# A hybrid decoder step on one core: low-part products over all 128 partitions

## The chip, the core and the metric

The kernel runs on one core of one Trainium2 chip. TensorE (PE) multiplies, VectorE (DVE), ScalarE (ACT) and GpSimd (POOL) work on elements, and SyncE (SP) issues most transfers between DRAM and on-chip memory (SBUF). Each engine takes its instructions in a fixed order and waits on semaphores for the others. The metric is the device time of one execution in microseconds (us).

## The reference

One layer of a decoder with two parallel branches, for a prompt of 1024 tokens and 8 x 8 sample tokens that share the weights, all in float32, width 1024:

```
h = rmsnorm(x); p = h @ w_in
q, k, v, ga, ps, gb, ma, mb = split(p)
# branch A: attention, 16 heads of 64 in 4 key groups, window 128, bias by distance, one sink per head
s = q k^T * 64**-0.5 + bias (masked);  o = softmax with sink (s) v
ya = (o * silu(ga)) @ w_out_a
# branch B: RWKV-7, 16 heads of 64
z = ps + (prev - ps) * mu;  r, k, v, wl, al = split(z)
w_raw = -softplus(-(w0 + tanh(wl) @ w2)) - 0.5        # rank 64
a     = sigmoid(a0 + al @ a2)                          # rank 64
per token:  S = S * decay + (S at) bt + v k;  y = S r
yb = (groupnorm(y) + bonus) * silu(gb) @ w_out_b
out = rmsnorm(x + (sigmoid(ma) * ya + sigmoid(mb) * yb) @ w_o)
```

Key and value windows, the RWKV states and the last shifted rows are returned too.

## The kernel before

Channels lie on the 128 partitions and tokens along the free axis, in chunks of 364, 364 and 360 columns. A float32 operand is split into a high part that the fast matmul format (fp32r) holds exactly and a low part, the rest. A dense product takes three passes into one PSUM region: high by high, high by low, low by high (`mm3`, shown as `d` in the profile: `whi`, `wlo` are the weights' parts, `hhi`, `hlo` those of h, `yhi`, `ylo` those of the RWKV output, `oh`, `ol` those of the attention output).

The program has these stages. `start` norms the input, with constants loaded through POOL's queue: `con` (identity, epsilons, masks, scan pattern, all in one tile of 728 columns), `prm` and others. `rwkv` runs about 16 units of 256 tokens by two groups of heads: `quarter` does the element work of a group (`lo`, `kn`, `bo`, `A`, `t` products), `invert` a triangular inversion on DVE (`TM`, `TR`, `Tt`), `chain` the recurrence (`c`, `y`, `q` products), `samples` the sample tokens (`ss`; `ve` is a masked copy for the state update, made with the scan constants of `con`), `posts` the group norm (`gc` with the centring matrix `cen`, `gv` with the block sums `bone`). Dense projections fill PE between them. `attention` follows, and `final` does the output projections (`wo`).

The order on PE is written by a planner (`drive`): each stream is a generator that stops before products that must wait; the planner keeps an estimated clock, advanced in `mm` by columns alone, and goes on with the first stream whose operands should be there. Dense products are the last stream and fill the rest. Within the RWKV stage and within attention this order is kept on PE; the other engines' orders, and how the end of one stage mixes with the start of the next, come from the framework's scheduler. Buffers are tiles of pools laid out in SBUF end to end in the order in which the pools open: constants, weights, then RWKV elements, chain and post; the attention pools open where the RWKV pools stood. A tile that takes the place of others waits for their last use.

*Attention.* For a pair of heads (e = 0, 1, one on each half of the partitions) `att_keys` loads the keys `kT` and writes for each head a tile `ks` with the high part of its keys on both halves (ACT, L1027 and L1028), and one tile `klo` with the low parts, each head's in place on its own half (DVE, L1029). `q_split` makes for each head a tile `qs` with the query's high part on the head's half and its low part on the other. Thus one product over 128 rows gives (q high + q low) times k high, and a second over the 64 rows of the head's half adds q high times k low. `att_half` runs 2 blocks of 128 queries at a time: eight score products (`s`), softmax on DVE and ACT (`sc`, with the eviction from PSUM at L1126, the exponential at L1052, the scaling at L1056), transposes (`pt`), products with values (`o`, values by token in `vtok`, made by the transposes `vt` of `vT`), and the gate. Two halves of the blocks run as separate streams, for eight pairs of heads.

*Low-rank projections.* The tiles `zs` hold for each token the rank-64 vector's high part on one half of the partitions and its low part on the other; the weights `w2` stand twice, on both halves, and are split into `w2h` and `w2l`. One product over 128 rows takes w2h with both parts, a second over the 64 rows of the high part adds w2l with it.

Of the kernel before, what the change touches and what calls it, by code (L numbers as in the profile page):

```python
# [42 lines left out]
# tile numbers in the stacked weight array  # L43
# [11 lines left out]
# columns of the shape constants  # L55
C_ID = 0
C_MI = 128
C_MS = 192
C_SI = 256
C_SS = 320  # L60
C_SEQ = 384
C_SCAN = 392
C_EPS = 724
NCONST = 728

# columns of the per-channel parameters
# [15 lines left out]
class Prog:  # L82
# [6 lines left out]
    # ---------------------------------------------------------------- helpers  # L89
# [6 lines left out]
    def cst(self, col, n, lo=0, hi=P):  # L96
        return self.con[lo:hi, col:col + n]

    # ---------------------------------------------------------------- PE order
    def mm(self, out, lhsT, rhs, transpose=False, **kw):  # L100
        """a product, and its estimated time"""
        n = 1
        for d in rhs.shape[1:]:
            n *= d
        if transpose:
            self.nc.tensor.transpose(out, lhsT, rhs)  # L106
        else:
            self.nc.tensor.matmul(out, lhsT=lhsT, rhs=rhs, **kw)  # L108
        self.clk += n / 2400 if rhs.dtype == F32R else n / 1200 if lhsT.shape[-1] > 64 else n / 1700
# [22 lines left out]
    def ready(self, st):  # L132
        """estimated time at which a stream's next products have their operands"""
        if st[2] is not None:
            if st[2] not in self.marks:
                return None
            st[2], st[3] = None, self.marks[st[2]] + st[3]
        return max(st[3], self.free.get(st[4], 0.0))

    def drive(self, streams):  # L140
        """products are issued in the order of emission: of the streams (generators that stop ahead of products
        that have to wait for other engines) the first one whose operands should be there goes on"""
        live = [[gen, off, None, 0.0, None] for gen, off in streams]
        while live:
            best = None
            for st in live:
                t = self.ready(st)
                if t is not None and (best is None or t < best[0] - 1e-9) and not (best and best[0] <= self.clk):
                    best = (t, st)
            assert best, ("no stream can go on", [(st[0].__name__, st[2]) for st in live], self.marks.keys())  # L150
            t, st = best
            self.clk = max(self.clk, t)
            if not self.step(st):
                live.remove(st)
# [17 lines left out]
    def chunk_tiles(self, stack, nm):  # L172
        """hi and lo parts of a [P, KT, NT] operand, a pool for each chunk"""
        hi, lo = [], []
        for c0, c1 in CHUNKS:
            pool = stack.enter_context(self.pool(f"{nm}{c0}", side="right"))
            hi.append(pool.tile([P, KT, c1 - c0], F32R, name=f"{nm}hi{c0}"))
            lo.append(pool.tile([P, KT, c1 - c0], F32R, name=f"{nm}lo{c0}"))
        return hi, lo
# [20 lines left out]
    def dense2(self, ia, ib, rhi, rlo, ea, eb):  # L200
        """two tiles, chunk by chunk"""
        wa = self.pre.pop(ia)
        self.seq.remove(ia)
        self.seq.remove(ib)
        wb = self.load_w(ib)
        for ci, (c0, c1) in enumerate(CHUNKS):
            for j, (i, w, evac) in enumerate(((ia, wa, ea), (ib, wb, eb))):
                ps = self.ps(self.d3, f"d{i}_{ci}") if (2 * ci + j) % 3 == 2 else self.ps("d", f"d{i}_{ci}", 2)
                yield from self.mm3(ps[:, :c1 - c0], *w, rhi[ci], rlo[ci])
                evac(c0, c1, ps[:, :c1 - c0])  # L210
                if ci == 2 and j == 0:
                    self.pre[self.seq[0]] = self.load_w(self.seq[0])
                yield

    def sig_neg(self, out, tmp, src, scale, bias):
        """out = sigmoid(-(scale*src + bias)), by exp and ln of one table set"""
        nc = self.nc
        nc.scalar.activation(tmp, src, AF.Exp, scale=scale, bias=bias)
        nc.scalar.activation(tmp, tmp, AF.Ln, bias=1.0)
        nc.scalar.activation(out, tmp, AF.Exp, scale=-1.0)  # L220

    def load_split(self, pool, src, hi, lo, nm, bufs):
        """exact hi/lo parts of a float32 row of tiles in DRAM"""
        nc = self.nc
        t = pool.tile([P, NT], F32, tag="stage", name=f"stage{nm}", bufs=bufs)
        nc.sync.dma_start(t, src)
        nc.scalar.activation(hi, t, AF.Copy)  # L227
        nc.vector.tensor_tensor(lo, t, hi.bitcast(F32), ALU.subtract)  # L228
# [8 lines left out]
    def sum2(self, ps, w, parts):  # L237
        """ps = w^T (hi + lo) with w exact in fp32r: one pass for each part"""
# [3 lines left out]
    # ---------------------------------------------------------------- program  # L242
    def run(self):
        tc, nc = self.tc, self.nc
        nc.scalar.preload_act_table_set("natural_log_exp_and_others")
        with ExitStack() as top:
# [16 lines left out]
            self.con = cp.tile([P, NCONST], F32, name="con")  # L263
            self.prm = cp.tile([P, NPAR], F32, name="prm")
            self.prd = cp.tile([P, 52], F32, name="prd")
            self.bone = cp.tile([P, P], F32R, name="bone")
            self.cen = cp.tile([P, P], F32R, name="cen")
# [12 lines left out]
    def start(self, xp, w0):  # L280
        """the norm, chunk by chunk, with the first two projections"""
# [5 lines left out]
        self.zs = [ep.tile([P, NT], F32R, name=f"zs{j}") for j in range(2)]  # L287
        bc = xp.tile([P, 2, P], F32, name="bc")
        for t, i in ((self.con[:, C_MI:], self.I["con"][:, C_MI:]), (prm, self.I["par"]), (self.con[:, :C_MI], self.I["con"][:, :C_MI]),
# [95 lines left out]
    # ------------------------------------------------------------------ RWKV  # L385
    def shift_tile(self, idx, ti, out):
        """project one token-shifted tile; out(ci, c0, c1, z) takes z = ps + (prev - ps) * mu by chunks"""
# [49 lines left out]
    def spill(self, idx, dst, kind="copy", scale=1.0):  # L437
        """a projected tile, or its sigmoid or silu, sent to DRAM"""
# [105 lines left out]
    def front(self, s):  # L544
        """unit s: 256 tokens (and, with the last of them, the sample tokens) of two groups of two heads"""
# [31 lines left out]
    def quarter(self, g, q, gi, f):  # L577
# [10 lines left out]
        def v64(t):  # prompt chunks  # L588
            return t[:, :256].rearrange("p (c s) -> p c s", c=4)

        def s64(t):  # sample tokens by sequence
            return t[:, 256:320].rearrange("p (b s) -> p b s", b=NB)

        def d64(t, off, w=64):  # decay layout, prompt; off 1 = inclusive, 0 = exclusive
# [13 lines left out]
        # decay and in-context rate  # L608
        res = []
        pl = [self.ps("m", f"lo{nm}0"), self.ps("a", f"lo{nm}1", 2)]  # L610
        for j, r0 in enumerate((0, 64)):
# [3 lines left out]
            self.mm(ps[:, :n], lhsT=w2[1][r0:r0 + 64, j, :], rhs=self.zs[j][r0:r0 + 64, a0:a0 + n], start=False, stop=True)  # L615
# [18 lines left out]
        # normalised key  # L634
# [4 lines left out]
        # k' = k * (1 + (a - 1) * k_a)  # L639
# [18 lines left out]
        # bonus: v * sum(r * k' * r_k)  # L658
# [10 lines left out]
        # chunk arrays  # L669
# [67 lines left out]
    def invert(self, nm, n2, f):  # L737
        """tr[0:64] = ((I - A_ab)^-1)^T: 32 x 32 diagonal blocks by forward substitution, then merged.
        A block's columns lie on three partitions (columns 3c', 3c'+1, 3c'+2)."""
# [188 lines left out]
    # ------------------------------------------------------------- attention  # L928
# [46 lines left out]
    def att_load(self):  # L975
        """values by token, keys, and queries that were projected before"""
# [41 lines left out]
    def att_keys(self, m):  # L1018
        """keys of a pair of heads: hi parts on both halves of the partitions, lo parts in place"""
# [4 lines left out]
        self.klo = self.a0.tile([P, SEQ], F32R, tag="klo", name=f"klo{m}", bufs=1)  # L1024
        for e in range(2):
# [3 lines left out]
            nc.vector.tensor_tensor(self.klo[er], t[er, :SEQ], self.ks[e][er].bitcast(F32), ALU.subtract)  # L1029
# [5 lines left out]
    def q_split(self, qs, src, c0, c1, scale):  # L1035
        """queries: a head's hi parts on its half of the partitions, its lo parts on the other half"""
# [6 lines left out]
    def softmax4(self, sc, mx, sinkv, nu, nm, x):  # L1043
        """sc: [P, nu, w] scores with bias, mx: [P, nu] row maxima (sink included); normalised in place"""
# [44 lines left out]
    def att_half(self, x):  # L1089
        """half of the blocks of each pair of heads"""  # L1090
# [5 lines left out]
        for i in QORD:  # L1096
# [7 lines left out]
            for b0 in range(bq, bq + 4, 2):  # L1104
# [7 lines left out]
                for e in range(2):  # L1112
                    er = slice(e * 64, e * 64 + 64)
                    for bb in range(2):
# [6 lines left out]
                        self.mm(po, lhsT=qs[e][er, b * P:(b + 1) * P], rhs=self.klo[er, k0:k0 + w], start=False, stop=True)  # L1121
# [105 lines left out]
    # ---------------------------------------------------------------- output  # L1227
# [92 lines left out]
# ------------------------------------------------------------- host layouts  # L1320
def _chan(v, n):
    """[n*128] per-channel vector -> [128, n]"""
# [9 lines left out]
def _consts():  # L1332
# [22 lines left out]
    # block ones; block centering  # L1355
# [4 lines left out]
def prep(inp):  # L1360
# [45 lines left out]
    # [(twice, rank), g, decay | rate, channel]  # L1406
# [3 lines left out]
    # [b, h, v, k] -> [g, (h2, k), b, v]  # L1410
# [7 lines left out]
    # sample: rows (b4, g, i); columns 128 cached + 64 new (b, i)  # L1418
# [28 lines left out]
def finish(r):  # L1447
# [4 lines left out]
    def win(a):   # [m, (e, d), t] -> [t, kv, d]  # L1452
# [5 lines left out]
    # [g, k, (h2, v)] -> [h, v, k]  # L1458
    pw = np.ascontiguousarray(r["pwkv"].reshape(8, 64, 2, 64).transpose(0, 2, 3, 1)).reshape(1, 1, 16, 64, 64)
    # [g, (h2, k), b, v] -> [b, h, v, k]  # L1460
# [19 lines left out]
```

## Time and profile before

| | |
|---|---|
| time, median of 3 runs | 1918.33 us (1914.55 to 1920.26) |
| profiled execution, first to last instruction | 1909.7 us |
| PE busy | 1837.7 us (96%) |
| PE weight loads busy | 1617.2 us (85%) |
| DVE busy | 1117.7 us (59%) |
| ACT busy | 968.6 us (51%) |
| POOL busy | 359.6 us (19%) |
| mean granted PE clock | 0.991 |

The page of the profile has the span of the profiled execution, not a device time of its own; the runs lie 4.9 to 10.6 us above the span. A row of a group reads: line, engine, operation, out<-in, shapes, count, then total busy us, mean ns of one, and idle time of the engine before them. A row of the timeline reads: start, length, engine, line, operation, tiles, shapes, count. In shapes such as `64*128` the first number is the rows of the array that a product contracts over, the second its output rows. `PEld` rows are weight loads, which can run under products. Records of products overlap, so their starts tell the pace.

### The profile page before, as it was taken

Reading aid. Unit: us, or ns where it says so; the run is one execution under the profiler, and the core shown is the slowest. Engines: PE = TensorE matmul, PEld = TensorE weight load, DVE = VectorE, ACT = ScalarE, POOL = GpSimd, SP = SyncE. Lnnn points to the kernel's source line nnn. Section 1 sums busy time; section 2 is a strip of 40 time slices with the busy share of each in tenths; the row PEclk is TensorE's granted clock in tenths of the full one; section 3 lists DMA queues with packets and bytes.
Section 4 is the critical chain, followed back from the end, with each engine's and each line's share of the span. In section 5 each row is a group of like instructions: output and inputs, shape, how many; then the busy total and the mean of one; then the engine's idle time right before and its main releaser. Section 6 shows DMA issues by size and latency. Waiting matters only on the chain.

```text
span 1909.7 us, 35535 instructions
## 1 busy us (share of the span) xinstructions
PE 1837.7 (96%) x13056; PEld 1617.2 (85%) x13056; DVE 1117.7 (59%) x3243; ACT 968.6 (51%) x2442; POOL 359.6 (19%) x356
## 2 busy tenths in 40 slices
PE   6999999999999999999999999999999999999998
PEld 4998888888787888887888888897888888799997
DVE  6325757576567466577576567544555666544543
ACT  5456556464455563565564555434555754432232
POOL 4443222132133212123211021211100000000000
PEclk9999999999999999999999999999999999999999
DMA  4333332332333333242332332332411524274521
GB/s 157 110 115 118 101 80 87 104 103 85 92 98 91 96 84 92 74 123 81 102 100 80 94 116 77 103 93 90 152 51 50 171 92 123 78 234 138 180 104 59
DMA packets 180994, 199.42 MB, mean 104 GB/s; under 512 B 72052, under 2 KB 156388, under 8 KB 180788
## 3 DMA queue, kind: packets, MB, share of 16 engines
q1 hardware_dynamic: 180244, 194.19, 33.7%
q0 software_dynamic: 576, 2.96, 0.5%
q8 instruction: 103, 1.69, 0.4%
q14 instruction: 71, 0.58, 0.1%
HBM read 135.09 MB, written 63.95 MB: 104 GB/s over the span
## 4 chain that ended last, share of the span: by engine, by line
PE 46%; DVE 3%; ACT 1%; DMA 1%; issue 1%; POOL 0%; DVEq 0%; SPq 0%; POOLq 0%; ACTq 0%
PE d L108 24%; PE wo L108 5%; PE s L108 4%; PE y L108 2%; PE c L108 2%; PE o L108 2%; PE pt L106 1%; DMA stageo<-d_o 1%; DVE Tt L757 1%; PE A L108 1%; DVE TR L759 1%; PE t L106 0%; PE lo L108 0%; PE os L108 0%; PE ss_d L108 0%
## 5 line engine op out<-in xcount | busy, mean ns | idle before, releaser
L108 PE MATMUL d<-hhi,whi 128*128 128x364 f32 (+1 forms) x1656 | 571.3, 345 | 9.4 <-DVE gz L432 5.4
L108 PE MATMUL d<-hlo,whi 128*128 128x364 f32 (+1 forms) x1656 | 549.3, 332 | 7.9 <-DVE hlo L347 7.0
L108 PEld LDWEIGHTS d<-hhi,whi 128*128 128x128 f32 x1656 | 315.3, 190 | 31.9 <-issue 9.2
L108 PE MATMUL d<-hhi,wlo 128*128 128x364 f32 (+1 forms) x1656 | 333.4, 337 | 0.0
L108 PEld LDWEIGHTS d<-hlo,whi 128*128 128x128 f32 x1656 | 315.8, 191 | 11.3 <-DVE hlo L347 9.6
L108 PEld LDWEIGHTS d<-hhi,wlo 128*128 128x128 f32 x1656 | 276.8, 190 | 9.6 <-issue 4.5
L169 POOL TENSOR_TENSOR wlo<-wraw,whi 128x1024 fp32r<-128x1024 f32 x56 | 136.0, 2429 | 360.9 <-PE d L108 136.5
L757 DVE TENSOR_TENSOR Tt<-TM,TR 96x90 f32<-96x90 f32 (+26 forms) x496 | 150.2, 303 | 11.0
L759 DVE TENSOR_TENSOR TR<-TR,Tt 96x90 f32<-96x90 f32 (+26 forms) x496 | 133.7, 270 | 13.7 <-issue 1.2
L168 ACT ACTIVATE whi<-wraw 128x1024 fp32r<-128x1024 f32 x90 | 95.0, 1056 | 79.0 <-PE d L108 70.5
L402 POOL TENSOR_TENSOR zz<-zz,pad 128x364 f32<-128x364 f32 (+1 forms) x75 | 76.1, 1016 | 204.9 <-ACT zz L401 139.7
L1052 ACT ACTIVATE sc<-sc,st 128x256 f32<-128x256 f32 (+1 forms) x128 | 61.9, 486 | 50.0 <-DVE st L1048 50.0
L830 DVE COPY vsu<-c 64x256 f32<-64x256 f32 x64 | 27.4, 428 | 98.1 <-PE c L108 87.6
L108 PE MATMUL y<-am,vsu 128*64 128x64 f32 x512 | 81.4, 245 | 0.0
L108 PE MATMUL y<-tr,xs 64*64 64x64 f32 x480 | 77.9, 242 | 0.0
L1126 DVE CUSTOM_DVE_ANT_0 sc<-s,bias,prm 128x256 f32<-128x256 f32 (+1 forms) x128 | 55.7, 463 | 32.8 <-PE s L108 32.7
L400 ACT ACTIVATE pad<-d,prm 128x364 f32<-128x364 f32 (+1 forms) x75 | 40.8, 544 | 60.3 <-PE d L108 50.8
L1314 POOL TENSOR_TENSOR xr<-xr,frs 128x256 f32<-128x256 f32 x2 | 1.8, 932 | 368.0 <-ACT frs L1311 368.0
L108 PE MATMUL d<-yhi,whi 128*128 128x364 f32 (+1 forms) x192 | 65.0, 339 | 0.0
L108 PE MATMUL d<-oh,whi 128*128 128x364 f32 (+1 forms) x192 | 63.4, 330 | 0.7 <-ACT oh L227 0.5
L108 PE MATMUL d<-ol,whi 128*128 128x364 f32 (+1 forms) x192 | 63.2, 329 | 0.4 <-DVE ol L228 0.4
L108 PE MATMUL A<-RA,KB 64*128 64x128 f32 x544 | 63.5, 291 | 0.0
(308 smaller groups left out, 3626.6 us busy)
## 6 DMA issues: line engine op xcount, KB each, us to landing
wraw<-in_w SPq DMA_DIRECT2D x93, 512.0 KB
d_z<-zz SPq DMA_DIRECT2D x48, 182.0 KB
d_m<-sp SPq DMA_DIRECT2D x32, 182.0 KB
TM<-s SPq DMA_DIRECT2D x72, 64.0 KB
stageo<-d_o SPq DMA_DIRECT2D x8, 544.0 KB
d_z<-zz SPq DMA_DIRECT2D x24, 180.0 KB
w<-in_lora SPq DMA_DIRECT2D x32, 128.0 KB
bias<-in_biasp SPq DMA_DIRECT2D x16, 256.0 KB
```

Source lines behind the costliest of these rows:

```text
L106: self.nc.tensor.transpose(out, lhsT, rhs)
L108: self.nc.tensor.matmul(out, lhsT=lhsT, rhs=rhs, **kw)
L168: nc.scalar.activation(hi, raw, AF.Copy)
L169: (nc.vector if self.dve_lo else nc.gpsimd).tensor_tensor(lo, raw, hi.bitcast(F32), ALU.subtract)
L400: nc.scalar.activation(pad[:, 1:1 + m], ps[:, :m], AF.Copy, scale=mu)
L402: nc.gpsimd.tensor_tensor(z[:, :m], z[:, :m], pad[:, 0:m], ALU.add)
L757: nc.vector.tensor_tensor(tv, M[s // 16][:np_, s % 16:s % 16 + 1, s + 1:32].to_broadcast([np_, cc, w]), R[:np_, 0:cc, s:s + 1].to_broadcas ...
L759: nc.vector.tensor_tensor(R[:np_, 0:cc, s + 1:32], R[:np_, 0:cc, s + 1:32], tv, ALU.add)
L830: nc.vector.tensor_copy(vsu[up, c], pu)
L1052: nc.scalar.activation(sc[k], sc[k], AF.Exp, bias=st[:, 0, k:k + 1], accum_out=st[:, 1, k:k + 1])
L1126: nc.vector.tensor_tensor_reduce(sc[:, k, off:], ps[e][:, bb * 256 + off:bb * 256 + 256], bias[:, e, off:], 1.0, self.par(Q_SK + 4 * i + k ...
L1314: en.tensor_tensor(xt[:, dt, :n], xt[:, dt, :n], rst[:, :n], ALU.mult)
```

## The change

- The low keys get a tile for each head, `klo[e]`, with the low part on both halves of the partitions, and the second score product contracts over all 128 partitions of `qs[e]` and `klo[e]`.
- The second low-rank product contracts over all 128 partitions of `w2l` and `zs`.
- `con` keeps only the identity and the epsilons. Masks and scan constants move to a tile `rco`, and `rco`, `bone` and `cen` are now in the pool of RWKV elements, which ends with the RWKV stage. The order of the constant loads is `con`, `prm`, `rco`.

Comments and docstrings are dropped too. The core of the diff:

```diff
 C_ID = 0
-C_MI = 128
...
-C_SCAN = 392
-C_EPS = 724
+C_EPS = 128
+C_MI = 132
...
+C_SCAN = 396
 NCONST = 728
...
     def cst(self, col, n, lo=0, hi=P):
-        return self.con[lo:hi, col:col + n]
+        if col < C_MI:
+            return self.con[lo:hi, col:col + n]
+        return self.rco[lo:hi, col - C_MI:col - C_MI + n]
...
-            self.con = cp.tile([P, NCONST], F32, name="con")
+            self.con = cp.tile([P, C_MI], F32, name="con")
...
-            self.bone = cp.tile([P, P], F32R, name="bone")
-            self.cen = cp.tile([P, P], F32R, name="cen")
...
+        self.rco = ep.tile([P, NCONST - C_MI], F32, name="rco")
+        self.bone = ep.tile([P, P], F32R, name="bone")
+        self.cen = ep.tile([P, P], F32R, name="cen")
...
-        for t, i in ((self.con[:, C_MI:], self.I["con"][:, C_MI:]), (prm, self.I["par"]), (self.con[:, :C_MI], self.I["con"][:, :C_MI]),
+        for t, i in ((self.con, self.I["con"][:, :C_MI]), (prm, self.I["par"]), (self.rco, self.I["con"][:, C_MI:]),
                      (bc, self.I["bc"]), (self.shp, self.I["shift"])):
...
-        for j, r0 in enumerate((0, 64)):
+        for j in range(2):
...
-            self.mm(ps[:, :n], lhsT=w2[1][r0:r0 + 64, j, :], rhs=self.zs[j][r0:r0 + 64, a0:a0 + n], start=False, stop=True)
+            self.mm(ps[:, :n], lhsT=w2[1][:, j, :], rhs=self.zs[j][:, a0:a0 + n], start=False, stop=True)
...
-        self.klo = self.a0.tile([P, SEQ], F32R, tag="klo", name=f"klo{m}", bufs=1)
+        self.klo = [self.a0.tile([P, SEQ], F32R, tag=f"klo{e}", name=f"klo{m}{e}", bufs=1) for e in range(2)]
         for e in range(2):
...
-            nc.vector.tensor_tensor(self.klo[er], t[er, :SEQ], self.ks[e][er].bitcast(F32), ALU.subtract)
+            for r in (er, xr):
+                nc.vector.tensor_tensor(self.klo[e][r], t[er, :SEQ], self.ks[e][er].bitcast(F32), ALU.subtract)
...
-                        self.mm(po, lhsT=qs[e][er, b * P:(b + 1) * P], rhs=self.klo[er, k0:k0 + w], start=False, stop=True)
+                        self.mm(po, lhsT=qs[e][:, b * P:(b + 1) * P], rhs=self.klo[e][:, k0:k0 + w], start=False, stop=True)
```

More of the change, by code (lines that the diff above doesn't have):

```diff
@@ L56 @@
 C_ID = 0
-C_MI = 128
[L58 to L61, printed above, removed]
-C_SCAN = 392
-C_EPS = 724
+C_EPS = 128
+C_MI = 132
+C_MS = 196
+C_SI = 260
+C_SS = 324
+C_SEQ = 388
+C_SCAN = 396
 NCONST = 728
@@ L1112, in att_half @@
                 for e in range(2):
-                    er = slice(e * 64, e * 64 + 64)
                     for bb in range(2):
```

## The prediction

> **What bounds the kernel now.** I read the totals first, then the busy time by stage, then the groups by shape, and last the instructions in order of time.
>
> ```profile
> span 1909.7 us, 35535 instructions
> ...
> PE 1837.7 (96%) x13056; PEld 1617.2 (85%) x13056; DVE 1117.7 (59%) x3243; ACT 968.6 (51%) x2442; POOL 359.6 (19%) x356
> ```
>
> TensorE (PE) is occupied almost throughout and nothing else passes 60%. The stages say the same (columns: window, length, busy of PE, weight load, DVE, ACT, POOL, granted clock, DMA share, GB/s):
>
> ```profile
> 1000.00:1270.00 270.00, 265.11 (x2078) 229.73 (x2078) 165.03 (x499) 143.93 (x360) 51.83 (x47) 0.99 0.32 92
> ...
> 1340.00:1500.00 160.00, 158.98 (x1026) 135.75 (x1025) 89.41 (x328) 88.26 (x250) 3.54 (x5) 1.00 0.26 83
> ...
> 1670.00:1800.00 130.00, 128.86 (x778) 126.96 (x777) 63.57 (x98) 33.05 (x44) 0.00 (x0) 1.00 0.58 175
> ```
>
> So PE sets the time in the RWKV stage (to about 1340 us), in attention (1340 to 1672) and behind it, and a microsecond taken off PE's own sequence is a microsecond of the span unless another engine is late. What matters is therefore the distance between starts on PE, not the length of a record, since records overlap. Three groups by shape, then the attention scores of one step in order of time:
>
> ```profile
> L108 PE MATMUL s<-ks,qs 128*128 128x256 f32 x112 | 42.8, 382 | 0.0
> L108 PE MATMUL s<-klo,qs 64*128 64x256 f32 x112 | 42.6, 381 | 0.0
> ...
> L108 PE MATMUL gc<-shic,cen 128*128 128x256 f32 x24 | 6.8, 284 | 0.0
> ```
>
> ```profile
> 1407.33 0.39 PE L108 MATMUL o<-pt,vtok 128*64 128x128 f32 x4
> 1407.64 0.38 PE L108 MATMUL s<-ks,qs 128*128 128x256 f32 x1
> 1407.96 0.38 PE L108 MATMUL s<-klo,qs 64*128 64x256 f32 x1
> 1408.27 0.39 PE L108 MATMUL s<-ks,qs 128*128 128x256 f32 x1
> ...
> 1409.83 0.38 PE L108 MATMUL s<-klo,qs 64*128 64x256 f32 x1
> 1410.14 1.09 PE L106 MATMUL pt<-con,sc 128*128 128x128 f32 x8
> ```
>
> Eight score products take 2.50 us, 0.31 each. A product of the same 256 columns, also in two passes into one PSUM region, but with 128 rows in both passes, starts the next one after 0.12:
>
> ```profile
> 1257.34 0.28 PE L108 MATMUL gc<-shic,cen 128*128 128x256 f32 x1
> 1257.46 0.28 PE L108 MATMUL gc<-sloc,cen 128*128 128x256 f32 x1
> 1257.57 0.33 PE L108 MATMUL d<-hhi,whi 128*128 128x364 f32 x1
> ```
>
> The weight loads show why. The first two rows are loads of the scores, the others of that pair:
>
> ```profile
> 1407.95 0.18 PEld L108 LDWEIGHTS s<-klo,qs 64*128 64x128 f32 x1
> 1408.27 0.19 PEld L108 LDWEIGHTS s<-ks,qs 128*128 128x128 f32 x1
> ```
>
> ```profile
> 1257.34 0.19 PEld L108 LDWEIGHTS gc<-sloc,cen 128*128 128x128 f32 x1
> 1257.46 0.19 PEld L108 LDWEIGHTS d<-hhi,whi 128*128 128x128 f32 x1
> ```
>
> The load of gc's second pass begins at 1257.34, as the first pass starts: it is hidden. The load of a score's 64-row pass begins at 1407.95, 0.31 behind the start of the product before it: nothing overlaps. This happens at each change between 128 and 64 rows, in both directions.
>
> **The change part by part.** *Scores.* The low pass takes 128 rows instead of 64, so the alternation ends. The columns streamed stay 256 (the added rows add the product of the two low parts), and I take 0.12 for a step. The first step after the o products (64 columns wide, still another shape) keeps an exposed load. That price is seen here, where kn follows a 64-row product:
>
> ```profile
> 110.16 0.28 PE L108 MATMUL lo<-zs,w2h 128*128 128x256 f32 x1
> 110.37 0.38 PE L108 MATMUL lo<-zs,w2l 64*128 64x256 f32 x1
> 110.68 0.38 PE L108 MATMUL lo<-zs,w2h 128*128 128x256 f32 x1
> 110.99 0.38 PE L108 MATMUL lo<-zs,w2l 64*128 64x256 f32 x1
> 111.30 0.39 PE L108 MATMUL kn<-shik,bone 128*128 128x256 f32 x1
> 111.53 0.28 PE L108 MATMUL kn<-slok,bone 128*128 128x256 f32 x1
> ```
>
> kn's first pass takes 0.23 to the next start. A group of eight then takes 0.23 + 7 x 0.12 = 1.07 instead of 2.50; the full-row product behind it loses its own exposed load, 0.23 - 0.12, so 1.5 us per group. There are 32 groups (8 head pairs x 2 halves x 2). In 8 of them four of the eight products have 128 columns, for the first block of tokens:
>
> ```profile
> 1637.75 0.33 PE L108 MATMUL s<-ks,qs 128*128 128x128 f32 x1
> 1638.00 0.32 PE L108 MATMUL s<-klo,qs 64*128 64x128 f32 x1
> ```
>
> These step by 0.25 now, and I take 0.11 after (the pt row above: 8 transposes of 128 columns, 1.09 with the last one's 0.27 in it), which leaves 1.3. Sum: 24 x 1.5 + 8 x 1.3 = 46.4 us. Bounds: 0 if the load stays exposed, 32 x 1.6 = 51 if the first step came down too.
>
> *Low-rank projections.* From the first lo to kn's second pass are 1.37 us; five steps at 0.12 make 0.60. That is 0.77 for each of 32 quarters (8 groups x 4; a quarter of them has 320 columns, for which I take the same), 24.6 us. Bounds 0 and 26.
>
> *How much arrives at the end.* In attention, softmax has to lie between scores and transposes, and a shorter PE sequence eats its slack. Normalising one step's scores (DVE) ends here, against its transposes on PE, once early and once late in attention:
>
> ```profile
> 1401.54 1.14 DVE L1056 TENSOR_SCALAR sc<-sc,st 128x256 f32<-128x256 f32 x4
> ```
>
> ```profile
> 1648.62 0.55 DVE L1056 TENSOR_SCALAR sc<-sc,st 128x128 f32<-128x128 f32 x2
> ```
>
> ```profile
> 1649.81 0.38 PE L106 MATMUL pt<-con,sc 128*128 128x128 f32 x2
> ```
>
> Early, the result is there at 1402.68 and used at 1410.14, over 7 us later; the 1.4 us of one group between them is covered. Over the last two heads (from about 1628, six groups) the last result is made at 1649.17 and used at 1649.81: 0.6 of cover. There the step loses up to 1.4, but DVE also starts its evictions earlier, since both PSUM banks are full after 1.07 rather than 2.5 while four evictions of 0.48 follow; I charge half, 6 x 0.7 = 4 us (0 to 9). What is late next there is the DVE eviction with ACT's exponentials. In the RWKV stage PE does wait, some 35 us in pieces, the largest in total being (in total, times, longest)
>
> ```profile
> PE t L106 <- ACT vsu L734: 10.9, 4, 3.8
> ```
>
> These are local hand-overs that move along with PE; the chain from lo through ACT also begins 0.6 us earlier. I keep 9 tenths, 22 us (15 to 25).
>
> *Second low key tile.* Four more DVE subtractions:
>
> ```profile
> L1029 DVE TENSOR_TENSOR klo<-kT,ks 64x1024 fp32r<-64x1024 f32 x4 | 4.8, 1209 | 0.6 <-ACT ks L1027 0.5
> ```
>
> 4 x 1.21 = 4.8 us on DVE, two at about 1330 and two at about 1497. DVE is 56% busy in that stretch. At 1330 the last RWKV post-processing stands behind them on DVE, and PE's gv waits for it, so up to 2.4 us may show; without that neighbour nothing would.
>
> *Memory.* The constants' pool shrinks by 2384 + 1024 bytes a partition (RWKV columns of con, bone, cen) and the pool of RWKV elements grows by as much, so its other tiles stay where they were. Attention's first pool begins where the elements began, 3.4 KB lower, and its tiles now lie over other RWKV tiles. By the order of allocation, the first value stage (bytes 8448 to 12800) comes to lie on the RWKV masks and scan constants, which the last sample step (ve) still reads, and ks of head 0 (12800 to 16896) on bone and cen, which the last gv reads:
>
> ```profile
> 1312.89 0.52 SPq L983 DMA_DIRECT2D vT<-d_v  x1
> ```
>
> ```profile
> 1331.88 0.67 DVE L893 TENSOR_TENSOR ve<-vss,con 128x512 f32<-128x512 f32 x1
> ```
>
> ```profile
> 1338.07 0.60 PE L106 MATMUL vt<-con,vT 128*128 128x128 f32 x4
> ...
> 1341.62 0.41 PE L108 MATMUL gv<-slov,bone 128*128 128x320 f32 x1
> ```
>
> The load can go at 1332.6 instead of 1312.9, and the transposes want it at 1338.07: 5.5 us for issue and 544 KB, which may just do. Behind it on the SyncE queue stand weight loads and the biases. ks of head 0 would be written from 1342 on, four operations of 1.1 to 1.2 us before its scores at 1353: covered. I charge 2 us for this and the DVE work together (a gain of 1 to a loss of 8).
>
> *Start.* The first constants' load falls from 300 to 66 KB, the third grows to 298 KB; the same bytes move.
>
> ```profile
> 14.64 0.56 ACT L330 ACTIVATE rst<-ss,con 128x364 f32<-128x364 f32 x1 [1.04 <-PE ss L108]
> ```
>
> prm may come a little earlier, but the first user that PE sees is rst, which waits for PE and not for constants: nothing (0.5 either way). The masks are first used after 100 us.
>
> Sum: 46.4 - 4 + 22 - 2 = 62 us. The profiled span would be 1909.7 - 62 = 1848. The runs' median, 1918.33, is 8.6 over that span, launch and spread together, which I leave as it is: 1918 - 62 = 1856.
>
> **The rivals.** *A: softmax takes over.* PE's share of attention falls by 46 of 332 us, and DVE with ACT become the limit in more than the last two heads. For it: the late rows above. Against: 7 us of cover earlier, and DVE and ACT at 55 to 56%; the same work in 138 instead of 160 us is 65%. If half of the attention gain goes, and RWKV keeps 15: 1918 - 23 - 15 = 1880, between 1876 and 1900.
>
> [...]
>
> *C: slower, by the clock.* The score and low-rank stretches draw full-array work at more than twice the rate. The granted clock is 0.99 to 1.00 in the windows above; if the denser stream brought it below about 0.96, PE's 1700 us of full-rate work would lose the 62 us again, and at 0.94 the kernel would take 1918 - 62 + 0.06 x 1700 = 1958. Against: from 1670 to 1800 PE does nothing but 128-row products, weight loads busy 98%, at 1.00.
>
> **How the numbers follow.** Forecast as summed, gains of 42 to 78 us, 0.82; A 0.12; B 0.03; C 0.03. The upper gain, 78, is all of the two terms with their upper bounds; the lower end takes the unfavourable end of each charge (46 - 9 + 15 - 8 = 44). The range 1840 to 1876 holds the forecast's case. A difference under 0.3% (6 us) cannot be told from none here, as the three runs spread by 5.7. Faster: forecast and A, 0.94; same: B, 0.03; slower: C, 0.03.
>
> **What would show it.** Right: s and lo products all 128 rows with mean records near 0.28 us, starts 0.12 apart, PE busy near 1775, DVE up by 5, klo eight times. Attention shorter by 40 or more between its first score and its last o, RWKV by about 20. [...] Wrong it would be through a long PE wait between 1310 and 1355 of the old time (value stage, ks, or a weight load stuck behind them), or steps between 0.12 and 0.31.

## The result, and the profile after

The changed kernel takes 1870.51 us (median of four runs, 1865.87 to 1874.02) against 1918.40 for the kernel before; the ratio is 0.9745, with an interval of 0.9717 to 0.9772. That is 48 us less where 62 were forecast, and the time lies within the predicted range, 14 us above the forecast of 1856. Some 12 us are lost at one place, the hand-over from RWKV to attention (experiment 3 measures it).

The totals of the profiled execution, which took 1874.02 us:

```profile
span 1872.2 us, 35547 instructions
...
PE 1783.7 (95%) x13056; PEld 1610.3 (86%) x13056; DVE 1123.9 (60%) x3247; ACT 963.8 (51%) x2442; POOL 359.2 (19%) x356
```

The changed products as groups by shape:

```profile
L110 PE MATMUL s<-ks,qs 128*128 128x256 f32 x112 | 31.4, 309 | 0.0
L110 PE MATMUL s<-klo,qs 128*128 128x256 f32 x112 | 28.3, 281 | 0.0
...
L110 PE MATMUL lo<-zs,w2l 128*128 128x256 f32 x48 | 12.6, 285 | 0.0
...
L1033 DVE TENSOR_TENSOR klo<-kT,ks 64x1024 fp32r<-64x1024 f32 x8 | 10.3, 1288 | 1.7 <-ACT ks L1030 1.5
```

Eight scores in order of time, with the dense product behind them:

```profile
1404.91 0.38 PE L110 MATMUL s<-ks,qs 128*128 128x256 f32 x1
1405.13 0.28 PE L110 MATMUL s<-klo,qs 128*128 128x256 f32 x1
1405.25 0.28 PE L110 MATMUL s<-ks,qs 128*128 128x256 f32 x1
...
1405.96 0.33 PE L110 MATMUL d<-hhi,whi 128*128 128x360 f32 x1
```

The records are down to 0.28 us except for the first ones, and the starts lie 0.12 apart; the first step, behind another shape, takes 0.22. The group takes 1405.96 - 1404.91 = 1.05 us (2.50 before, 1.07 forecast). So the products do what the prediction said. The hand-over does not. The stretch around it (columns: window, length, busy PE, weight load, DVE, ACT, POOL, granted clock, DMA share, GB/s), first after, then before:

```profile
1270.00:1320.00 50.00, 50.00 (x430) 39.66 (x429) 15.45 (x30) 13.77 (x32) 1.04 (x1) 1.00 0.18 55
1320.00:1340.00 20.00, 12.58 (x49) 9.92 (x48) 10.21 (x15) 11.64 (x21) 11.62 (x13) 0.74 0.50 151
1340.00:1360.00 20.00, 18.44 (x121) 17.73 (x120) 12.22 (x33) 8.30 (x21) 0.00 (x0) 1.00 0.83 279
```

```profile
1320.00:1340.00 20.00, 20.00 (x125) 15.98 (x123) 13.26 (x23) 12.00 (x22) 2.75 (x3) 1.00 0.31 103
1340.00:1360.00 20.00, 18.98 (x107) 16.55 (x106) 9.24 (x28) 10.08 (x25) 3.54 (x5) 1.00 0.77 251
```

After, TensorE stands still for 7.4 of 20 us and its clock is at 0.74 in that window; before, it worked throughout at 1.00. What it waits for, in order of time, after:

```profile
1325.32 0.31 PE L110 MATMUL gc<-sloc,cen 128*128 128x320 f32 x1
1329.74 0.60 PE L110 MATMUL gv<-shiv,bone 128*128 128x320 f32 x1 [4.11 <-DVE ysb L914]
1330.53 0.64 PE L110 MATMUL gv<-slov,bone 128*128 128x320 f32 x1 [0.18 <-DVE slov L236]
1333.98 0.67 PE L110 MATMUL d<-hhi,whi 128*128 128x364 f32 x1 [2.82 <-DVE qs L1045]
1334.45 0.51 PE L110 MATMUL d<-hlo,whi 128*128 128x364 f32 x1
1334.76 0.51 PE L110 MATMUL d<-hhi,whi 128*128 128x364 f32 x1
...
1343.53 0.66 PE L108 MATMUL vt<-con,vT 128*128 128x128 f32 x4 [1.43 <-DVE vtok L995]
```

The same place before:

```profile
1336.51 0.42 PE L108 MATMUL gc<-shic,cen 128*128 128x320 f32 x1
1336.77 0.33 PE L108 MATMUL d<-hlo,whi 128*128 128x364 f32 x1
1336.93 0.32 PE L108 MATMUL d<-hhi,whi 128*128 128x364 f32 x1
...
1337.76 0.31 PE L108 MATMUL gc<-sloc,cen 128*128 128x320 f32 x1
```

gc and gv are the norm of the last RWKV unit, two products with a chain over DVE and ACT between them. Before, dense products (d) of attention's query projection run between them and hide the chain. After, no dense product stands between gc and gv, so the chain is bare (4.11 us), and the next ones wait behind gv for the eviction of queries (2.82 us). And the dense products that follow start 0.31 apart (1334.45 and 1334.76), not 0.16 as before (1336.77 and 1336.93): half clock (0.50 in the windows of experiment 9). The SyncE queue shows attention's first loads at the back as well; before, `kT<-d_k` was issued at 1312.42, after:

```profile
1324.06 0.35 SPq L903 DMA_DIRECT2D out_swkv<-sin  x1
...
1330.53 0.42 SPq L929 DMA_DIRECT2D d_y<-ysb  x1
1331.00 0.42 SPq L1025 DMA_DIRECT2D kT<-d_k  x1
```

The keys' load now stands behind the last unit's outputs, though its own bytes lie on `zs`, as they did before, and are long free.

One of the five runs of experiment 9 below was slow (2216.34 us at a clock of 0.704, against 0.981 to 0.986 in the others) and does not count in its time.

### The profile page after: what moved, and what is told of

Its sections match the earlier page's. It is cut to its first block, busy times and chain, and to the rows that moved or that the text cites. A ratio compares the mean times of both kernels' runs of the same rounds, so it can differ in the third digit from the quotient of the medians.

```text
span 1872.2 us, 35547 instructions
## 1 busy us (share of the span) xinstructions
PE 1783.7 (95%) x13056; PEld 1610.3 (86%) x13056; DVE 1123.9 (60%) x3247; ACT 963.8 (51%) x2442; POOL 359.2 (19%) x356
## 4 chain that ended last, share of the span: by engine, by line
PE 43%; DVE 3%; DMA 2%; issue 1%; ACT 1%; POOL 0%; SPq 0%; DVEq 0%; POOLq 0%; ACTq 0%
PE d L110 24%; PE wo L110 5%; PE y L110 2%; PE c L110 2%; PE s L110 2%; PE o L110 2%; PE pt L108 1%; PE A L110 1%; DMA mb<-d_m 1%; DVE Tt L760 1%; DMA d_w<-mb 1%; DVE klo L1033 0%; PE os L110 0%; PE t L108 0%; PE ss_d L110 0%
## 5 line engine op out<-in xcount | busy, mean ns | idle before, releaser
L110 PE MATMUL d<-hhi,whi 128*128 128x364 f32 (+1 forms) x1656 | 574.6, 347 | 14.8 <-DVE gz L435 7.9
L110 PE MATMUL d<-ylo,whi 128*128 128x364 f32 (+1 forms) x192 | 64.1, 334 | 0.0
```

## The experiments

Theory M: the change of memory moves attention's first work behind the last RWKV unit. Rival F: the last unit's chain sets a floor there in any case, and what TensorE saves in RWKV ahead of it is lost. Rival K: a lower granted clock, from the denser stream. Ratios are to runs of before on the same chip.

| kernel | time, us | ratio to before (interval) | clock, median |
|---|---|---|---|
| before, the 17 runs beside experiments 1 to 4 | 1918.95 | | 0.987 |
| 1 low-rank products alone | 1901.7 | 0.9904 (0.9881 to 0.9927) | 0.985 |
| 2 memory alone | 1929.48 | 1.0045 (1.0029 to 1.0062) | 0.984 |
| 3 changed, constants at the other end | 1853.3 | 0.9647 (0.9628 to 0.9666) | 0.985 |
| 4 changed kernel again | 1869.11 | 0.9735 (0.9711 to 0.9758) | 0.982 |
| 5 as 3, scores alone | 1873.41 | 0.9775 (0.9746 to 0.9804) | 0.987 |
| 6 before, scores in pairs | 1891.27 | 0.9849 (0.9824 to 0.9873) | 0.986 |
| 7 changed, constants behind the elements | 1868.71 | 0.9737 (0.9718 to 0.9756) | 0.982 |
| 8 as 3, but bone and cen among the elements | 1867.8 | 0.9735 (0.9716 to 0.9754) | 0.981 |
| 9 changed, with filling products (four runs) | 1867.22 | 0.9729 (0.9707 to 0.9752) | 0.984 |
| 10 changed, half of klo on GpSimd | 1869.48 | 0.9749 (0.9727 to 0.9771) | 0.982 |
| 11 as 3, half of klo on GpSimd | 1861.1 | 0.9699 (0.9679 to 0.9718) | 0.982 |
| 12 as 3, again | 1854.34 | 0.9667 (0.9651 to 0.9684) | 0.984 |

**1. The low-rank products alone.** The kernel before with

```diff
-            self.mm(ps[:, :n], lhsT=w2[1][r0:r0 + 64, j, :], rhs=self.zs[j][r0:r0 + 64, a0:a0 + n], start=False, stop=True)
+            self.mm(ps[:, :n], lhsT=w2[1][:, j, :], rhs=self.zs[j][:, a0:a0 + n], start=False, stop=True)
```

> Only the low-rank products are changed (128 rows in both passes); scores, low key tile, constants and their loads are those of before. Theory M (the change of memory holds attention's first loads back and costs about 11 us at the hand-over from RWKV to attention): the low-rank gain of 12 to 22 us reaches the end, time 1898 to 1906 against 1918. Rival F (the last unit's chain sets a floor at the hand-over, so what PE saves in RWKV is lost there whatever lies where): 1914 to 1918, with PE idle growing between 1300 and 1355. Rival K (the granted clock falls with the denser stream): the clock is lower than that of before by about 0.004 and the time is 1906 to 1912.

17 us less by the medians, 18 by the ratio. The hand-over is intact (window view):

```profile
1320.00:1340.00 20.00, 18.97 (x116) 17.68 (x115) 11.16 (x20) 11.29 (x23) 6.38 (x7) 1.00 0.57 174
```

Rival F falls: what RWKV saves does reach the end.

**2. The memory alone.** The changed kernel's constants (`rco`, `bone`, `cen` in the pool of elements, loads in the new order) with the old products and one low key tile:

```diff
-            self.con = cp.tile([P, NCONST], F32, name="con")
-            self.bone = cp.tile([P, P], F32R, name="bone")
-            self.cen = cp.tile([P, P], F32R, name="cen")
+            self.con = cp.tile([P, C_MI], F32, name="con")
...
+        self.rco = ep.tile([P, NCONST - C_MI], F32, name="rco")
+        self.bone = ep.tile([P, P], F32R, name="bone")
+        self.cen = ep.tile([P, P], F32R, name="cen")
```

> Only the memory is changed: constants of RWKV in the pool of elements, loads in the new order; all products and the low key tile are those of before. Theory M: 8 to 13 us slower than before, 1926 to 1931, the keys' first load issued behind the last unit's output, PE idle around 1330 to 1355. Rivals F and K: 1916 to 1920, as before.

8.7 us slower by the ratio (5.6 to 11.9). TensorE's longest waits there, and the window:

```profile
PE gv L110 <- DVE ysb L914: 4.1, 1, 4.1
PE d L110 <- DVE qs L1044: 2.8, 1, 2.8
```

```profile
1340.00:1360.00 20.00, 14.19 (x71) 13.08 (x72) 9.33 (x15) 12.16 (x23) 9.25 (x11) 0.74 0.83 248
```

The same two waits of 4.1 and 2.8 us and the same clock of 0.74, with none of the new products. So the waits and the half clock come from the memory, and K, which blames the products, falls for this place.

**3. The constants at the other end of memory.** The changed kernel with

```diff
-                with self.pool("elem") as self.ep:
+                with self.pool("rwc", side="right") as self.rp, self.pool("elem") as self.ep:
...
-        self.rco = ep.tile([P, NCONST - C_MI], F32, name="rco")
+        self.rco = self.rp.tile([P, NCONST - C_MI], F32, name="rco")
```

and the same for `bone` and `cen`. They are as short-lived as in the changed kernel, but no early tile of attention lies on them.

> The changed kernel with the three constant tiles in a pool of their own at the other end of memory, so that no early attention tile lies on them; products as in the changed kernel. Theory M: 8 to 12 us faster than the changed kernel, 1858 to 1863, the keys' first load back ahead of the last unit's output. Rivals F and K: 1867 to 1874, as the changed kernel.

15.8 us less than the changed kernel beside it, more than expected. Between 1305 and 1370 us only one wait of 0.6 us is left, and the keys' load is early again (waits, then the SyncE queue):

```profile
PE gv L110 <- DVE ysb L914: 0.6, 1, 0.6
```

```profile
1306.29 1.18 SPq L860 DMA_DIRECT2D out_pwkv<-so  x2
1307.52 0.58 SPq L1025 DMA_DIRECT2D kT<-d_k  x1
```

The same 9606 products stand on TensorE ahead of the first score in each of these kernels, so its start measures the hand-over. It is 1336.91 here and 1351.07 in experiment 4; 1.4 us of that lie ahead of the hand-over, so that the hand-over costs 12.8 us. In experiment 2 against before it is 1365.34 against 1353.05, with 2.2 us ahead of it: 10.1 us.

**4. The changed kernel beside the others.**

> The changed kernel once more, on the same chip as the others: 1866 to 1874 by every theory. Rival K: its granted clock is below that of before by 0.005 or more in most runs, and its time goes with it; theory M alone: the clock is as likely above as below.

Its clock is 0.982 in the median, that of before 0.987. Over the 17 runs of before (from 0.981 and 1925.28 us to 0.991 and 1913.47 us) 0.001 of clock goes with about 1 us, by a line through them. By this line the clock is worth some 5 us against before, and 3 against experiment 3 (0.985). The first part of K's expectation is met, its cause is not, as 2 and 3 show.

**5. The scores alone**, with the memory of 3 and the old low-rank products.

> The kernel with the constants at the other end of memory, but with the old low-rank products (64 rows in the second pass): the score products alone are changed. If the two parts add up, 1853 + 18 = 1871, between 1867 and 1876 (the low-rank part alone was worth 17 us). Rival A (softmax takes part of the score gain): it would have shown in the run with both parts already, so here it can only show as a time above 1876, if the low-rank part and the scores share a gain.

45 us less than before by the medians (38 to 49 by the ratio). Low-rank and scores add up: 17.3 + 45.4 = 62.7 against 65.7 for both in 3. Rival A, softmax, takes nothing that shows.

**6. The scores in another order.** The kernel before; for each block, both heads' full passes and then both 64-row passes:

```diff
-                for e in range(2):
-                    er = slice(e * 64, e * 64 + 64)
-                    for bb in range(2):
...
-                        self.mm(po, lhsT=qs[e][er, b * P:(b + 1) * P], rhs=self.klo[er, k0:k0 + w], start=False, stop=True)
+                    for po, e, er in todo:
+                        self.mm(po, lhsT=qs[e][er, b * P:(b + 1) * P], rhs=self.klo[er, k0:k0 + w], start=False, stop=True)
```

> The kernel before, with the score products issued in another order: the full-row passes of both heads, then the two 64-row passes (rows 0 to 63, then 64 to 127), for one block after the other; same products, same memory. Theory S (a step costs 0.31 instead of 0.12 where the number of rows changes, and only there): of eight steps two full to full at 0.12, four changes at 0.31, two from 64 rows to 64 other rows at 0.12; 1.72 instead of 2.50 us a group, 32 groups with 0.7 us, 1918 - 22 = 1896 (1892 to 1901). Rival R (any 64-row product is dear, before and behind it): the two steps between 64-row products also take 0.31, 2.1 us a group, 1918 - 12 = 1906 (1903 to 1909). Rival X (the price is that of the order within one PSUM region, two passes one behind the other): all steps 0.12, 1.0 us a group, 1875.

28 us less, more than any theory but X gave, and the steps say why (two 64-row products in the row with x2, then their two weight loads):

```profile
1410.11 0.39 PE L108 MATMUL s<-ks,qs 128*128 128x256 f32 x1
1410.33 0.28 PE L108 MATMUL s<-ks,qs 128*128 128x256 f32 x1
1410.54 0.38 PE L108 MATMUL s<-klo,qs 64*128 64x256 f32 x2
1410.85 0.39 PE L108 MATMUL s<-ks,qs 128*128 128x256 f32 x1
```

```profile
1410.54 0.18 PEld L108 LDWEIGHTS s<-klo,qs 64*128 64x128 f32 x2
```

The two 64-row products, on rows 0 to 63 and 64 to 127, together take 0.31 (1410.54 to 1410.85), as one of them did before: they run side by side. The four products take 0.74 us (1410.11 to 1410.85); with the pair as one step, three steps without a change of row count would be 0.36, so that each of the two changes costs 0.19, just as 0.31 - 0.12 before. R falls, because a second 64-row product costs nothing here. X falls, because the changes still cost. S stands, but for its 0.12 between two 64-row products. The pair's two weight loads take 0.18 us together.

**7. The constants behind the elements.** As 3, but `self.pool("elem") as self.ep, self.pool("rwc") as self.rp`.

> The changed kernel with the three constant tiles in a pool of their own directly behind the elements. There they lie under attention's tile of values by token, which is first written at about 1340 us, when the last reader of the constants is done; the key and value stages and the key tiles lie on none of them. Theory H (the issue order, fixed when the program is built, puts all of attention's first work behind the last reader of what lies under an early attention tile, whether the bytes of a load are free or not): as the changed kernel, 1866 to 1872, with the keys' load behind the last unit's output. Rival O (at run time only those tiles wait that themselves lie on constants): 1851 to 1857.

No gain. The SyncE queue is that of the changed kernel:

```profile
1332.60 0.42 SPq L929 DMA_DIRECT2D d_y<-ysb  x1
1333.08 0.42 SPq L1025 DMA_DIRECT2D kT<-d_k  x1
```

`bone` and `cen` lie under the tile of values by token alone, which is first written behind the last gv anyway (the first 768 bytes of `rco` also lie under a later query tile); the tiles of keys, values and first queries lie where they lie in 3. And still keys, queries and dense products come late. So it is not a matter of the bytes that a load needs. Here as in the changed kernel the queue's order of issue has all of attention's start behind the last reader of the constants. By which of its rules the framework's scheduler does so, no trace shows.

**8. Only bone and cen among the elements.**

> The kernel with constants at the other end of memory, but with the two constant matrices of block sums and block centering (1 KB) back among the elements; masks and scan constants stay at the other end. If the masks (last read by the last sample step) cost the time, as the prediction had it for the value stage: 1851 to 1857. If the two matrices (last read by the last gv and gc products, some 10 us later) do: 1864 to 1872.

The whole loss comes back (1867.8), with 1 KB. The prediction had named the masks and the last ve as the longest obstacle; the two small matrices, which the last gc and gv read, are enough. They lie under the first value stage here and under ks in the changed kernel, with the same loss. The masks alone were not tried.

**9. The waits filled.** The changed kernel with

```diff
+        self.npost = getattr(self, "npost", 0) + 1
+        if self.npost == 32:
+            fill = self.ps("y", "fill0")
+            for _ in range(26):
+                self.mm(fill[:, :320], self.bone, self.hhi[0][:, 0, :320], start=True, stop=True)
...
         self.sum2(p2, self.bone, parts)
+        if self.npost == 32:
+            for _ in range(19):
+                self.mm(fill[:, :320], self.bone, self.hhi[0][:, 0, :320], start=True, stop=True)
```

> The changed kernel with 45 products added that nobody reads, 26 ahead of the last gv and 19 behind it, where TensorE waits 4.1 and 2.8 us at the hand-over; they run at 0.14 us each and go into a PSUM bank that is free there. Memory and order as in the changed kernel. Theory G (the half clock of 10.2 us at the hand-over is the answer to TensorE's waiting, and costs about 5 us of dense products at half rate): no half-clock spell between 1320 and 1345, first vt transposes 4 to 5 us earlier against the last gc product, time 1863 to 1867 against 1870. Rival I (the spell has another cause, such as the load of the dense stretch before it): the spell stays and the time is 1868 to 1874.

Half a hit. The granted clock over the place (window, length, busy PE, clock, DMA share, GB/s), first of the changed kernel, then of this one:

```profile
1325.00:1329.60 4.60, 0.56 (x2) 1.00 0.48 131
1329.60:1339.80 10.20, 7.05 (x21) 0.50 0.75 233
```

```profile
1326.00:1331.70 5.70, 3.20 (x20) 1.00 0.50 146
1331.70:1335.10 3.40, 3.24 (x11) 0.50 0.95 308
1335.10:1341.90 6.80, 4.76 (x31) 1.00 1.06 293
1341.90:1345.30 3.40, 3.40 (x14) 0.50 0.70 252
```

10.2 us at half clock became twice 3.4, each around the end of a wait that was left (below), so the spell follows the waiting. All six profiles with the wait of 4.1 us (of the changed kernel, and of 2, 4, 7, 8 and 10) have a spell of 10.24 us that begins 0.1 to 1.4 us before that wait ends (0.1 in the changed kernel: 1329.60 against 1329.74). The mean clock over the 20 us with the spell is 0.74 in five of them; in 7, where it lies in two such windows, 0.78 and 0.96. But the time moved by no more than can be told (1867.22 against 1869.11 and 1870.51):

```profile
PE d L110 <- DVE qs L1053: 2.3, 1, 2.3
PE vt L108 <- DVE vtok L1003: 2.0, 1, 2.0
```

G's other sign did not come: the first vt starts 15.0 us behind the last gc, against 13.8 in the changed kernel (14.4 in experiment 4). Two things are in the way. What TensorE did at half clock hardly fell, from 7.05 to 6.64 us. And ScalarE's order moved with the edit: it begins to evict the queries 3.0 us behind the start of the last gv product (1329.41), behind the rest of the norm, where the changed kernel does so after 1.1 us (1331.63). So the experiment shows what the spell follows, and not what its absence would save.

**10. Half of the low key subtractions on GpSimd**, in the changed kernel:

```diff
-            for r in (er, xr):
-                nc.vector.tensor_tensor(self.klo[e][r], t[er, :SEQ], self.ks[e][er].bitcast(F32), ALU.subtract)
+            for r, en in ((er, nc.vector), (xr, nc.gpsimd)):
+                en.tensor_tensor(self.klo[e][r], t[er, :SEQ], self.ks[e][er].bitcast(F32), ALU.subtract)
```

> The changed kernel, with the two added half subtractions of each pair of low key tiles on GpSimd instead of VectorE. If the block of four subtractions on VectorE holds up the copies of the values by token (TensorE waits 1.4 us for one of them at 1342): 1 to 4 us less, 1866 to 1869. If GpSimd's subtractions are the slower ones and ks or klo is late for the first scores: 1870 to 1876. In both cases the wait of vt for vtok goes away.

1869.48, no difference. The wait for vtok is gone, and one for the values' load has taken its place:

```profile
PE vt L108 <- DMA vT<-d_v: 2.6, 1, 2.6
```

As in 9, another wait stands behind the one taken away, from late loads and late evictions, and neither of the two tries gained anything that can be told.

**11. The same in the kernel of 3.**

> The same move to GpSimd in the kernel with the constants at the other end of memory. There dense products cover the hand-over, so VectorE's block costs nothing and the move gains nothing: 1851 to 1855. If it does gain there, 1850 or less, the block was on the path in that kernel too.

Neither: 1861.1, some 7 us slower than 3. GpSimd takes 2.36 and 2.69 us for the first two of these subtractions, where VectorE takes 1.2. While they run (1318.96 to 1324.09), VectorE is slow as well: ve takes 2.47 us instead of the 0.67 of 12, and a klo 3.38 instead of 1.21 (3.07 at most in 10). TensorE waits for that ve, and for sin, which stands behind that klo on VectorE:

```profile
PE ss_d L110 <- DVE ve L896: 1.6, 1, 1.6
PE gv L110 <- DVE sin L901: 1.0, 1, 1.0
```

Against the profile of 12, dense products come 3 us later at this place and another 2.8 us later at about 1650. A further 5.3 us lie ahead of 1315 us, where the code is the same; they stay open.

**12. The kernel of 3 again.**

> The kernel with the constants at the other end of memory once more. If its 1853 us is a property of the kernel and the 8 us that the move to GpSimd cost are a price of that move: 1850 to 1856. Rival: part of the 16 us against the changed kernel was a favourable run of half-clock spells in the RWKV stage, and the move to GpSimd cost nothing: 1858 to 1862.

1854.34: the gain is the kernel's own. It is the best version here, 3.3 to 3.5% under the kernel before, against 2.6% for the change as made.

## Why the prediction was right, and where its sum was off

*Score step and group: right.* 0.12 and 1.05 us against 0.12 and 1.07. 46.4 - 4 = 42.4 us were forecast, 45 measured in experiment 5, within its interval. The 4 us for softmax in the last two heads can't be told from none.

*Low-rank: right in size.* 22 forecast (15 to 25), 17 to 18 measured in experiment 1, with an interval of 14 to 23.

*Memory and second low key tile: the step that failed.* 2 us were charged, with 8 as the worst. Memory alone costs 8.7 us, and in the changed kernel the placement costs about 15 (15.8 against 3, 14.8 against 12). The range held the result all the same, because the other charges left room for it. Three links were missing. First, the prediction asked only which tiles themselves lie on the constants (the first value stage, ks of head 0), and counted their waits; but keys, queries and dense products moved too, though their bytes were free (7). Second, it named no cover for the chain of the last gc and gv. Before, dense products stood there (the rows of before under the result), and when these went, 4.1 + 2.8 us lay open, with 1.4 for vt behind them. Third, it counted a wait as its own length, while 10.2 us at half clock came on top. In them TensorE worked for 7.05 us, at full clock 3.5: an estimate of 3.5 us for the spell. Together that is 11.8 of the 12.8 us at the hand-over. Its warning, a long TensorE wait between 1310 and 1355, named the place and not the cause. By the times the loss in the changed kernel exceeds that of memory alone by some 7 us (15.8 against 8.7), by the first score only by 2.7 (12.8 against 10.1). Of these, vt's longer wait is one part (1.4 against 0.5); the rest stays open.

*Offset: wrong, but without effect on the difference.* The 8.6 us between the span of before and the median were put down to launch and spread. The device time lies 1.8 us above the span (1874.02 - 1872.2). The profiled execution of before ran at a clock of 0.991, the upper end of its 17 runs, for which the line of experiment 4 gives some 4 us; the other 3 are spread.

*VectorE and start: right.* VectorE is up by 6.2 us (5 forecast), and moving the four added subtractions to GpSimd gains nothing (10). From 100 to 335 us the products of memory alone start within 0.1 us of those of before.

*The rivals.* A did not happen. B, that the steps stay at 0.31 us and the time at 1918, did not: the score steps are 0.12, and the load of a full-row pass, 0.19 us long, runs under the full-row product ahead of it (in the changed kernel both begin at 1405.13). C's clock did fall, by 0.005, but about half of that goes with the waits and not with density: the clock is 0.984 to 0.985 in experiments 3 and 12, with the same products. The 0.002 to 0.003 that are left stay open.

Without the memory term the forecast's own terms give 1918.95 - 64.4 = 1854.5. The kernels without that loss measured 1853.3 and 1854.3. That the sum fits so well is partly luck: the scores gave 3 us more than forecast, and the low-rank products 5 less.

## What to carry to other kernels

Where scratch memory is reused from one stage to the next, a small tile that is read to the very end of the first stage should lie under nothing that the second stage needs early; ask for each moved tile who reads it last, and what work the order of issue then puts behind that reader. Price a wait on a saturated TensorE as the wait plus the half clock that can follow it (here an estimate of 3.5 us on 8.3 us of waits), and name the filler products that hide a chain before you cost the chain at nothing. Two passes with different numbers of rows should be made equal, or at least be grouped so that the row count changes seldom (a change cost 0.19 us here).

## What the runs showed of the hardware

The change from a 128-row to a 64-row product of 256 columns, or back, cost 0.19 us on top of a step of 0.12 (0.31 a step in the kernel before, and two changes in the 0.74 us of experiment 6), and two 64-row products on different halves of the rows ran side by side in 0.31 us (experiment 6).

In the profiles of before and after, the clock dropped to half in spells of 3.4, 6.8 and once 10.2 us (the last one of each profile runs past the span), mostly around the end of a wait of TensorE. In the kernel before, seven of the eight spells begin within 2 us of the end of a wait of 1.35 to 3.85 us; for instance (window, length, busy PE, clock, DMA share, GB/s):

```profile
183.70:186.50 2.80, 0.00 (x1) 1.00 0.60 187
186.50:187.10 0.60, 0.60 (x5) 0.96 0.00 0
187.10:190.50 3.40, 3.40 (x13) 0.50 0.46 141
```

Here the wait was 2.8 us. A wait does not settle it, though: in the same profile waits of 3.03 us (to 614.90) and 3.05 us (to 908.72) were followed by 7 us at a clock of 1.00. Nor does it take a wait: in the changed kernel the spells from 1493.44, 1517.34 and 1537.82 (a clock of 0.51 over the 3.5 us from 1493.40, 1517.30 and 1537.80) come behind 3.5 us at 1.00 in which the profile shows no wait of TensorE (busy for all of the 3.50 us), but small products of the sample tokens (`os`, `sm`). What decides between these cases stays open.

While GpSimd ran a subtraction of 64 x 1024 elements, two of VectorE's operations beside it took 2.8 and 3.7 times as long (experiment 11: 3.38 instead of 1.21 us, 2.47 instead of 0.67).
